# A two-network kernel in fp32: kmat's queue, the modulations' places, both convolutions' inverses, and a guard at the layer fronts

## The chip, the cores and the metric

The kernel runs as one launch on one core of a Trainium2 chip. The metric is the device time of that core in microseconds. The kernel before has a median of 1523.81 us over three runs (1521.16 to 1525.88).

## The reference

Two networks of two layers each follow one another on a sequence of 256 tokens of width 1024, all in fp32. Every layer has a mixer and a feed-forward part, each behind an RMS norm that is modulated by vectors (`sh`, `sc`, `g`) computed from a conditioning vector `c`.

```python
sh1, sc1, g1, sh2, sc2, g2 = split(silu(c) @ mod_w[i] + mod_b[i], 6)
h = modulate(rms_norm(x, norm_g), sh1, sc1)
x = x + g1 * mixer(h)
h = modulate(rms_norm(x, norm_g'), sh2, sc2)
x = x + g2 * ffn(h)

# network 1, layer 0: s5_mixer (state space) beside moba_attention, then @ ab_w_out
# network 1, layer 1: conformer_conv
def conformer_conv(h, w_in, b_in, dw_w, dw_b, ln_g, ln_b, w_out, b_out):
    a = h @ w_in + b_in
    a = a[..., :D_CONV] * jax.nn.sigmoid(a[..., D_CONV:])
    a = causal_dwconv(a, dw_w, dw_b)          # 31 taps
    a = jax.nn.silu(layer_norm(a, ln_g, ln_b))
    return a @ w_out + b_out
# network 2, layer 0: latent attention over the tokens and a context of 256 more
# network 2, layer 1: hyena_mixer
    y = (two_sided_fftconv(v, h_fwd, h_bwd) + v * d_bias) * x1
    return y @ w_out + b_out
```

## The kernel before, in words

Activations are kept transposed, as eight chunks of 128 channels by 256 tokens. Each weight arrives in tiles of 128x1024 fp32 (512 KB) and is split: ACT writes a rounded high part `hi` (L412), DVE the rest `lo` (L413). A product is then three matmuls, hi by hi, hi by lo and lo by hi (`mm3`, L434 to L436). A block of 128 output channels is 8 chunks by 3, so 24 matmuls of 256 columns. TensorE therefore works through blocks, each of which waits for its weight's two parts.

SP's queue loads the weights in a fixed order into pools of buffers (`raw` with five, and `raw2` where `more` opens a second pool). A load waits in that order until the tile that used its buffer has been split, and all loads behind it wait too. POOL's queue loads rows of a second form of the modulation weights (`modt`) into `mraw`, three buffers, for DVE, which forms products of a row by `c` (`also`, L506). The rest of the modulation is done by TensorE: `modulation` loads a tile of two 128-row slices and issues four matmuls on it into one bank `mo` (L532). The planner has lists of such pending steps (`later`), each with a cost, and the code around a block counts `done` upward (`behind`, `fill`, `need`); `pace` sets how often DVE's row products come.

Which instruction stands where on an engine is decided when the program is built: the tile framework orders them by a simulated schedule, and `tc.issue_after` forbids it to take an instruction before another one. On the chip each engine runs its order as written.

The stages, in the order of time, are: conditioning and input of the first network, with the state space `ssm` and its block matrix `kmat` (made in `ktab`, sent to DRAM as `kd`, read back as `kmat`), the attention heads and `ssm_out`, `ab_out`; `ffn1` (gate0, up0, down0); the convolution layer `layer_cm` (cm_in, a 256-point transform by matmuls, its inverse, cm_out); `ffn1` again; the context's operand and latent; `layer_mla`; `ffn2`; `layer_hy`; `ffn2`. A `Front` stands at the start of each layer: the first block is multiplied before the norm's scale is known, and `stats` supplies the scale through `rsqrt` (L633 to L638), a chain of eleven tiny DVE steps.

## Time and profile before

| what | value |
|---|---|
| median of 3 runs | 1523.81 us |
| profiled execution | 1522.47 us, its span 1520.7 us |
| granted TensorE clock over the span | 0.959 of full speed |
| PE busy | 1379.3 us (91%) |
| DVE busy | 1195.9 us (79%) |
| ACT busy | 839.3 us (55%) |
| POOL busy | 125.1 us (8%) |
| moved by DMA | 311.9 MB, 205 GB/s on the mean |

The profiled execution is 1.8 us longer than its span, and 1.3 us shorter than the median. Busy times of the engines overlap. The clock is the share of full speed (2.4 GHz) that was granted to TensorE: a stretch with 0.50 ran at 1.2 GHz.

### The profile page before, as it was taken

The numbers are of one execution on the slowest core, as the hardware profiler recorded it, in microseconds if no ns is written. First come the engines' busy times: TensorE is split into PE (matmuls) and PEld (weight loads), VectorE is DVE, ScalarE is ACT, GpSimd is POOL, SyncE is SP. The second block draws the span as 40 slices with busy tenths as digits, with TensorE's granted clock in tenths as the row PEclk, the third lists the DMA queues.
The fourth block names the chain that finished last, engine by engine and source line by source line (L and its number), as shares of the span: only waits on it lengthen the run. The fifth ranks groups of instructions, "written<-read, shape, count | busy, mean of one in ns | idle before, by whom it ended". The sixth has DMA issues, their size and how long they took to land.

```text
span 1520.7 us, 28172 instructions
## 1 busy us (share of the span) xinstructions
PE 1379.3 (91%) x10686; PEld 1249.7 (82%) x10686; DVE 1195.9 (79%) x2428; ACT 839.3 (55%) x1562; POOL 125.1 (8%) x166
## 2 busy tenths in 40 slices
PE   6969879999988689989987998989999999889997
PEld 3638779999973689989986877989998678889997
DVE  7958869978674678787968876899886979799954
ACT  5416466554452467554545765766545654676642
POOL 1000100101000000000100651000010000000000
PEclk9969989999999799998988999999999999999998
DMA  9476766878669246775835243467695664556651
GB/s 363 167 160 211 240 233 212 286 250 303 237 231 364 76 156 187 237 240 187 321 90 186 84 140 124 143 200 249 213 353 181 247 237 138 164 167 211 205 171 39
DMA packets 96214, 311.89 MB, mean 205 GB/s; under 512 B 14533, under 2 KB 18222, under 8 KB 95950
## 3 DMA queue, kind: packets, MB, share of 16 engines
q1 hardware_dynamic: 77054, 244.01, 48.7%
q0 software_dynamic: 17856, 65.02, 13.1%
q8 instruction: 84, 1.38, 0.4%
q10 hardware_dynamic: 1168, 1.06, 0.3%
q14 instruction: 52, 0.43, 0.1%
HBM read 308.73 MB, written 1.32 MB: 204 GB/s over the span
## 4 chain that ended last, share of the span: by engine, by line
PE 59%; issue 27%; DVE 6%; DMA 4%; ACT 2%; POOL 1%; SPq 0%; DVEq 0%; POOLq 0%; ACTq 0%
PE mm L434 16%; PE mm L436 16%; PE mm L435 16%; DVE lo L413 2%; PE o L1512 1%; POOL mraw L504 1%; DMA raw<-gate 1%; PE mo L532 1%; ACT hi L412 1%; PE ax L1612 1%; DMA kmat<-kd 1%; DVE mraw L506 1%; PE sx L1496 0%; PE s L434 0%; PE ax L1496 0%
## 5 line engine op out<-in xcount | busy, mean ns | idle before, releaser
L412 ACT ACTIVATE hi<-raw 128x1024 fp32r<-128x1024 f32 (+3 forms) x402 | 403.7, 1008 | 406.0 <-PE mm L435 285.3
L413 DVE TENSOR_TENSOR lo<-raw,hi 128x1024 fp32r<-128x1024 f32 (+3 forms) x402 | 465.3, 1161 | 167.0 <-ACT hi L412 161.8
L434 PE MATMUL mm<-hh,hi 128*128 128x256 f32 x1472 | 416.9, 287 | 16.4 <-DVE e L758 5.6
L436 PE MATMUL mm<-hh,lo 128*128 128x256 f32 x1472 | 415.5, 283 | 3.0 <-DVE lo L413 3.0
L435 PE MATMUL mm<-hl,hi 128*128 128x256 f32 x1472 | 414.9, 283 | 0.5 <-DVE hl L712 0.5
L434 PEld LDWEIGHTS mm<-hh,hi 128*128 128x128 f32 x1472 | 278.2, 190 | 26.0 <-issue 6.9
L435 PEld LDWEIGHTS mm<-hl,hi 128*128 128x128 f32 x1472 | 280.0, 190 | 5.1 <-DVE hl L712 2.0
L436 PEld LDWEIGHTS mm<-hh,lo 128*128 128x128 f32 x1472 | 279.8, 190 | 4.7 <-DVE lo L413 3.8
L434 PE MATMUL mm<-ah,hi 128*128 128x256 f32 x704 | 200.8, 286 | 1.5 <-ACT hi L412 1.5
L436 PE MATMUL mm<-ah,lo 128*128 128x256 f32 x704 | 198.6, 284 | 3.8 <-DVE lo L413 3.8
L435 PE MATMUL mm<-al,hi 128*128 128x256 f32 x704 | 198.3, 282 | 0.0
L434 PE MATMUL mm<-zh,hi 128*128 128x258 f32 x608 | 176.4, 295 | 20.6 <-ACT hi L412 10.9
L436 PE MATMUL mm<-zh,lo 128*128 128x258 f32 x608 | 176.2, 291 | 2.3 <-DVE lo L413 2.3
L435 PE MATMUL mm<-zl,hi 128*128 128x258 f32 x608 | 176.2, 291 | 0.0
L504 POOL DMA_DIRECT2D mraw<-modt x124 | 65.7, 530 | 1230.1 <-DVE mraw L506 1111.1
L506 DVE SCALAR_TENSOR_TENSOR mraw<-mraw,crow 128x1024 f32<-128x1024 f32 x124 | 149.9, 1219 | 6.3 <-DMA mraw<-modt 6.2
L434 PEld LDWEIGHTS mm<-zh,hi 128*128 128x128 f32 x608 | 118.9, 197 | 23.2 <-ACT hi L412 11.7
L436 PEld LDWEIGHTS mm<-ah,lo 128*128 128x128 f32 x704 | 132.6, 189 | 4.8 <-DVE lo L413 4.4
L434 PEld LDWEIGHTS mm<-ah,hi 128*128 128x128 f32 x704 | 133.3, 189 | 3.1 <-ACT hi L412 1.9
L435 PEld LDWEIGHTS mm<-al,hi 128*128 128x128 f32 x704 | 133.4, 190 | 1.0 <-issue 1.0
L436 PEld LDWEIGHTS mm<-zh,lo 128*128 128x128 f32 x608 | 119.7, 197 | 2.9 <-DVE lo L413 2.9
L435 PEld LDWEIGHTS mm<-zl,hi 128*128 128x128 f32 x608 | 120.6, 199 | 0.0
(416 smaller groups left out, 2076.4 us busy)
## 6 DMA issues: line engine op xcount, KB each, us to landing
raw<-up SPq DMA_DIRECT2D x132, 512.0 KB, 4.0
mraw<-modt POOLq DMA_DIRECT2D x124, 512.0 KB, 5.2
raw<-down SPq DMA_DIRECT2D x64, 512.0 KB, 4.6
raw<-mod SPq DMA_DIRECT2D x60, 512.0 KB, 6.2
raw<-gate SPq DMA_DIRECT2D x44, 512.0 KB, 4.7
raw<-down SPq DMA_DIRECT2D x32, 384.0 KB, 3.5
raw<-hy_in SPq DMA_DIRECT2D x24, 512.0 KB, 6.8
raw<-cm_in SPq DMA_DIRECT2D x16, 512.0 KB, 5.5
```

The lines of the kernel that those rows point to most:

```text
L412: nc.scalar.activation(hi, src, AF.Copy)
L413: return nc.vector.tensor_tensor(lo, src, hi.bitcast(F32), op=ALU.subtract)
L434: nc.tensor.matmul(out, wh, xh, start=start, stop=False)
L435: nc.tensor.matmul(out, wh, xl, start=False, stop=False)
L436: self.last = nc.tensor.matmul(out, wl, xh, start=False, stop=stop)
L504: nc.gpsimd.dma_start(w, self.d[f"modt{layer}"][u])
L506: nc.vector.scalar_tensor_tensor(w, w, 1.0, row, op0=ALU.mult, op1=ALU.mult, accum_out=out[:, u : u + 1]))
L532: nc.tensor.matmul(acc[g * 32 : g * 32 + 32, :], wt, src, start=(g not in begun), stop=last)
L1512: nc.tensor.matmul(o[i * 64 : i * 64 + 64], vals[:, k, c : c + 64], pt[i][:, k, :], start=(k == 0), stop=(k == 3))
L1612: nc.tensor.matmul(ps, m[:, k, m0 : m0 + P], src[:, k, s], start=(k == 0), stop=(k == 1))
```

## The change

- `kd` and `kmat` are sent through POOL's queue, and `ssm_out` is issued after the second pair of heads (`c == 1`) instead of the first, behind the last matmul.
- `more` gives the first five tiles behind it to the first pool, and the filter's loads are issued in the ninth feed-forward pair (`at={8: ...}`).
- The first `later` takes three column blocks instead of two (`range(4, 7)`) and DVE four rows fewer; `pace` and the end of a list reset the counters; the convolution's pairs, a `fill(3)` and the blocks of `down` take the modulations of the later layers.
- In `layer_cm` the transform is cut into `part` generators; parts 0 and 1 are issued behind the input blocks 5 and 7. The mean (`mu`) is not subtracted before the inverse but goes through it: three more matmuls per channel block use it as a broadcast operand. The inverse gives all 256 tokens in one PSUM tile half; z stays in PSUM, four banks.
- In `layer_hy` the inverse gives all 256 tokens from four matmuls of 256 columns instead of two halves of 128 that DVE adds and subtracts.
- `Front.guard` holds the splits of blocks 3 and 4 until the `rsqrt` chain is over.
- `ctx_operand` and `kv_latent` become steps that the feed-forward's pairs 15, 17 and 18 and the blocks of `down` call.
- `stats2` makes both scales in one `rsqrt` of four columns, and the positions' matmul is issued after the last matmul.

TensorE's order around the first matmul on `kmat`, before: `mo` is the modulation's bank and `qr`, `qi`, `X` belong to the state space.

```order
L532 MATMUL mo_1049<-raw_1058,cs_85 32x512 x2
L532 MATMUL mo_1049<-raw_1062,cs_85 32x512 x2
L532 MATMUL mo_1049<-raw_1066,cs_85 32x512 x2
L1089 MATMUL sx_1263<-kmat_867,u2_660 32x128 x4
L1092 MATMUL sx_1263<-qr_288,X_933 32x128 x4
L1092 MATMUL sx_1263<-qi_289,X_933 32x128 x4
```

The same place now; `ssb` is a head's probabilities, `hh` the input operand's high part.

```order
L449 MATMUL mm_1288<-hh_312,lo_1292 128x256
L547 MATMUL mo_1088<-raw_1324,cs_85 32x512 x2
L1216 MATMUL ax_1227<-ident_89,ssb_1214 128x128
L547 MATMUL mo_1088<-raw_1328,cs_85 32x512
L1216 MATMUL ax_1227<-ident_89,ssb_1214 128x128 x2
L547 MATMUL mo_1088<-raw_1328,cs_85 32x512
L1110 MATMUL sx_1396<-kmat_867,u2_660 32x128 x4
L1113 MATMUL sx_1396<-qr_288,X_933 32x128 x4
```

Five input blocks (118 of their matmuls), eight modulation tiles and the first heads' matmuls have moved ahead of it.

SP's order of weight loads between `ab_out` and the first feed-forward, before: `raw` and `raw2` are the two pools, `cmf` and `cmg` the convolution's matrices.

```order
L425 DMA raw_2130<-ab_out 128x1024
L425 DMA raw_2247<-up0 128x1024
L425 DMA raw_2345<-up0 128x1024
L425 DMA raw_2433<-up0 128x1024
L425 DMA raw_2521<-up0 128x1024
L425 DMA raw_2609<-up0 128x1024
L1252 DMA cmf_2185<-k_cm_f 128x384
L1254 DMA cmg_2187<-k_cm_g 128x320
L425 DMA raw2_2196<-gate0 128x1024
```

The same place now.

```order
L438 DMA raw_2134<-ab_out 128x1024
L438 DMA raw_2190<-gate0 128x1024
L438 DMA raw_2241<-up0 128x1024
L438 DMA raw_2273<-gate0 128x1024
L438 DMA raw_2339<-up0 128x1024
L438 DMA raw_2383<-gate0 128x1024
L438 DMA raw_2471<-gate0 128x1024
L438 DMA raw_2559<-gate0 128x1024
L438 DMA raw2_2427<-up0 128x1024
```

The first gate weight now follows `ab_out`'s last one at once, and the filter's loads stand a dozen loads later.

TensorE's order between the convolution's input and its inverse now: `cmat` and `cmau` are the transform's operands, `cmY` its result, `cmmu` the mean.

```order
L1334 MATMUL mm_5483<-cmat_4715,cmf_2877 128x128
L1343 MATMUL mm_5494<-cmau_4716,cmf_2877 128x128
L547 MATMUL mo_5413<-mraw_5497,cs_85 32x512 x2
L547 MATMUL mo_5413<-raw_5501,cs_85 32x512 x2
L547 MATMUL mo_5413<-raw2_5505,cs_85 32x512 x2
L547 MATMUL mo_5413<-mraw_5509,cs_85 32x512 x2
L547 MATMUL mo_5413<-raw_5513,cs_85 32x512 x2
L547 MATMUL mo_5413<-raw2_5517,cs_85 32x512 x2
L1363 MATMUL mm_5524<-cmg_2879,cmY_4718 128x256 x2
L1363 MATMUL mm_5524<-cmg_2879,cmY_4718 128x32
```

Before, 28 modulation tiles stood in one run ahead of the last input blocks of the convolution; six of them are here now, two before, the rest behind.

The diff, cut to its core:

```diff
--- before.py
+++ after.py
+    def guard(self):
+        return self.net.tc.issue_after(self.chain.ins) if self.n in (3, 4) else nullcontext()
     def block(self, ps, wh, wl, evac):
...
     def room(self):
+        if self.hold:
+            self.hold -= 1
+            return self.raw.tile([P, 1024], F32, name="raw")
         self.turn = (self.turn + 1) % len(self.raws)
...
             self.step()
+        if not self.pending:
+            self.done = 0.0
...
         self.sums(st, 2, sq2)
-        v1 = self.t([P, 2], "nv")
-        v.tensor_scalar(v1, st[:, 0:2], 1.0 / D, EPS, op0=ALU.mult, op1=ALU.add)
-        y1 = self.rsqrt(v1)
-        v2 = self.t([P, 2], "nv")
-        v.tensor_tensor(v2, y1, y1, op=ALU.mult)
...
-        y2 = self.rsqrt(v2)
-        v.tensor_tensor(y2, y2, y1, op=ALU.mult)
+        a = self.t([P, 4], "nv4")
+        v.tensor_scalar(a[:, :2], st[:, 0:2], 1.0 / D, EPS, op0=ALU.mult, op1=ALU.add)
+        v.tensor_scalar(a[:, 2:], st[:, 2:4], 1.0 / D, None, op0=ALU.mult)
+        v.scalar_tensor_tensor(a[:, 2:], a[:, :2], EPS, a[:, 2:], op0=ALU.mult, op1=ALU.add)
+        y = self.rsqrt(a, 4)
+        y1, y2 = y[:, :2], y[:, 2:]
         yield None
...
             self.raws.append((p, "raw2"))
+            self.hold = 5
             yield
...
-    def down(self, w, hi, lo, evac, every=1.0):
+    def down(self, w, hi, lo, evac, every=1.0, then=None):
         self.pace(every)
-        self.linear(w, range(Front.late), hi, lo, evac)
+        for m in range(Front.late):
+            self.linear(w, [m], hi, lo, evac)
+            if then:
+                self.behind(then)
         self.pace(1000.0)
...
         for q in range(4):
-            nc.sync.dma_start(kd[:, q, :, :].rearrange("s h m -> h s m"), kt[q * 32 : q * 32 + 16, :, :])
+            nc.gpsimd.dma_start(kd[:, q, :, :].rearrange("s h m -> h s m"), kt[q * 32 : q * 32 + 16, :, :])
         kmat = sp.tile([P, 32, P], F32, name="kmat")
...
         for j in range(8):
-            nc.sync.dma_start(kmat[j * 16 : j * 16 + 16, :, j * 16 :],
+            nc.gpsimd.dma_start(kmat[j * 16 : j * 16 + 16, :, j * 16 :],
                               kd.rearrange("s q h m -> h (s q) m")[:, :, : (8 - j) * 16])
...
                 cur = nxt
-                if c == 0:
-                    yc, yh, yl = self.ssm_out(sp, ap, u2)
+                if c == 1:
+                    with self.tc.issue_after(self.last.ins):
+                        yc, yh, yl = self.ssm_out(sp, ap, u2)
...
                 self.linear(d["cm_in"], [8 + j], hi, lo, gate)
+                if j in (5, 7):
+                    self.behind(parts[j == 7])
                 self.linear(d["cm_in"], [j], hi, lo, val)
-            for j in range(8):
-                pair(j)
+                if j in (5, 7):
+                    self.behind(parts[j == 7])
             Y = cp.tile([P, 3, D], F32, name="cmY")
-            parts = ((0, 512), (512, 896), (896, 1024))
...
+            def part(n, a, b):
                 s = slice(a, b)
-                vr, vi, vs = (self.mm()[:, : b - a] for _ in range(3))
-                for i, (q, x_) in enumerate(((vr, at[:, 1, s]), (vi, at[:, 0, s]), (vs, au[:, s]))):
-                    last = nc.tensor.matmul(q, cf[:, i, :], x_, start=True, stop=True)
+                vr, vi = (self.mm()[:, : b - a] for _ in range(2))
+                for i, (q, x_) in enumerate(((vr, at[:, 1, s]), (vi, at[:, 0, s]))):
+                    nc.tensor.matmul(q, cf[:, i, :], x_, start=True, stop=True)
...
                                            accum_out=su[:, i, n : n + 1])
+                yield
+                vs = self.mm()[:, : b - a]
+                self.last = nc.tensor.matmul(vs, cf[:, 2, :], au[:, s], start=True, stop=True)
                 v.scalar_tensor_tensor(Y[:, 2, s], vs, 1.0, H[:, 2, s], op0=ALU.mult, op1=ALU.mult,
                                        accum_out=su[:, 2, n : n + 1])
-            self.fill(2, last)
+                yield
+            parts = [part(n, a, b) for n, (a, b) in enumerate(((0, 512), (512, 896), (896, 1024)))]
+            for j in range(8):
+                pair(j)
+            for _ in parts[2]:
+                pass
+            self.fill(3, self.last)
...
             v.tensor_scalar(mu, mu, -1.0 / D, None, op0=ALU.mult)
-            for n in range(2):
-                s = slice(n * 512, n * 512 + 512)
-                for i in range(3):
-                    if (n + i) % 2:
-                        v.tensor_scalar(Y[:, i, s], Y[:, i, s], mu[:, i : i + 1], None, op0=ALU.add)
-                    else:
-                        nc.scalar.activation(Y[:, i, s], Y[:, i, s], AF.Identity, bias=mu[:, i : i + 1])
-            z = cp.tile([P, 8, T], F32, name="cmz")
+            zs = [z[:, i * T : i * T + T] for z in [self.mm() for _ in range(4)] for i in range(2)]
+            ins = ((0, slice(0, T), slice(0, T)), (1, slice(0, T), slice(T, 2 * T)), (2, slice(0, 32), slice(2 * T, 2 * T + 32)))
             q = []
             for j in range(8):
...
-                od = self.t([P, T], "eo", 2, pool=cp)[:, :P]
-                nc.scalar.activation(od, ps[:, :P], AF.Identity, bias=db[:, j : j + 1])
-                v.tensor_tensor(z[:, j, :P], ps[:, P:T], od, op=ALU.add)
-                v.scalar_tensor_tensor(z[:, j, : P - 1 : -1], ps[:, P:T], db2[:, j : j + 1], od, op0=ALU.add, op1=ALU.subtract)
-                self.sumsq(q, z[:, j, :], j, DC)
-            r = self.rstd(q, D, 1, 0)
+                for i, o, c in ins:
+                    nc.tensor.matmul(zs[j][:, o], Y[:, i, j * P : (j + 1) * P], cg[:, c], start=(i == 0), stop=False)
+                for i, o, c in ins:
+                    nc.tensor.matmul(zs[j][:, o], mu[:, i : i + 1].to_broadcast([P, P]), cg[:, c], start=False, stop=(i == 2))
+                self.sumsq(q, zs[j], j, DC, bias=db[:, j : j + 1])
+            r_ = self.rstd(q, D, 0, 2)
...
             zh, zl = self.operand()
...
             self.sumsq(cq, cx[k], k, DC, pool=cxp)
-        r = self.rstd(cq, D)
+        stats = self.stats(cq, D)
+        self.behind(stats)
+        yield
+        with self.tc.issue_after(self.last.ins):
+            r = next(stats)
         for k in range(DC):
             t = self.t([P, T], "n2", pool=cxp)
-            nc.vector.scalar_tensor_tensor(t, cx[k], gc[:, k : k + 1], r, op0=ALU.mult, op1=ALU.mult)
+            nc.vector.scalar_tensor_tensor(t, cx[k], g[:, k : k + 1], r, op0=ALU.mult, op1=ALU.mult)
             nc.scalar.activation(ch[:, k, :], t, AF.Identity, bias=sh[:, k : k + 1])
...
                 kp = self.ring("o")[:, s]
-                nc.tensor.matmul(kp, self.rsum[:64, :], pe[:64, s], start=True, stop=True)
+                with self.tc.issue_after(self.last.ins):
+                    nc.tensor.matmul(kp, self.rsum[:64, :], pe[:64, s], start=True, stop=True)
                 for i in range(4):
...
             for j in range(8):
-                ps = self.mm()
...
+                ps = self.mm()[:, :T]
+                for k in range(4):
+                    nc.tensor.matmul(ps, Y[:, k, j * P : (j + 1) * P], gg[:, k, :], start=(k == 0), stop=(k == 3))
                 y = self.t([P, T], "e")
-                od = self.t([P, P], "eo", 2, pool=hp)
-                nc.scalar.activation(od, pb, AF.Copy)
-                v.tensor_tensor(y[:, :P], pa, od, op=ALU.add)
-                v.tensor_tensor(y[:, : P - 1 : -1], pa, od, op=ALU.subtract)
-                v.tensor_tensor(y, y, x1[:, j, :], op=ALU.mult)
+                v.tensor_tensor(y, ps, x1[:, j, :], op=ALU.mult)
                 self.split(yh[:, j, :], yl[:, j, :], y)
...
                         pass
-            self.later(0, self.modulation(0, range(4, 6), cs, mods[:1]), 1.5)
+            self.later(0, self.modulation(0, range(4, 7), cs, mods[:1]), 1.5)
             row = self.row(0)
-            self.pace(1.2)
-            self.also(1, 0, 24, 40, row, mods[0])
+            self.pace(1.0)
+            self.also(1, 0, 28, 40, row, mods[0])
             self.p1 = per.tile([P, d["par1"].shape[1]], F32, name="p1")
...
-        self.ffn1(0, x, f, None, six(0, 5), sq, mid=mid, front=f2)
+        self.ffn1(0, x, f, None, six(0, 5), sq, mid=mid, front=f2, at={8: lambda: next(cm)})
         self.dump("x1", x)
...
         self.later(4, self.modulation(1, range(6, 9), cs, mods[1:2]), 2.5)
-        self.later(5, self.modulation(2, range(4), ("c_2", "c_ctx_2"), (mods[2], modc)), 5.0)
+        self.later(5, self.modulation(2, range(4), ("c_2", "c_ctx_2"), (mods[2], modc)), 2.0)
         self.pace(2.0)
...
                     self.also(7, 2, 24, 40, row2[0], mods[2])
-                    gc = self.gain("a2c", modc[:, 8:16], self.par("norm_mix_g_2", 0, 8))
-                    self.ctx_operand(cxp, ch, cl, gc, modc[:, 0:8])
-                    for _ in self.kv_latent(ch, cl, ckh, ckl, pe, 0, kv0, cxp, self.ax):
-                        pass
+                    next(latent)
+                    self.behind(latent)
...
                 with self.more(4):
-                    self.ffn1(1, x, f, None, six(1, 5), sq, sq2, lat, context, f2)
+                    self.ffn1(1, x, f, None, six(1, 5), sq, sq2, lat, context, f2, {j: lambda: next(ctx) for j in (15, 17, 18)}, latent)
```

## Rows read from the trace of the kernel before

**Rows 1.** busy us of each engine by stretch (us), then granted clock, DMA share, GB/s

```profile
0.00:1520.70 1520.70, 1379.29 (x10686) 1249.69 (x10686) 1195.94 (x2428) 839.30 (x1562) 125.12 (x166) 0.96 0.62 205
76.00:209.00 133.00, 103.37 (x930) 84.02 (x924) 93.67 (x226) 56.90 (x119) 9.76 (x18) 0.87 0.72 213
85.00:101.00 16.00, 1.01 (x12) 0.23 (x8) 9.40 (x35) 0.00 (x0) 0.00 (x0) 0.59 1.11 141
101.00:112.00 11.00, 11.00 (x114) 6.37 (x107) 3.23 (x3) 3.66 (x4) 0.00 (x0) 0.51 0.82 289
186.00:200.00 14.00, 4.06 (x19) 3.56 (x19) 9.27 (x19) 5.92 (x12) 2.66 (x5) 0.65 0.99 355
440.00:476.00 36.00, 27.89 (x147) 7.50 (x145) 7.99 (x28) 5.48 (x15) 1.58 (x3) 1.00 0.98 378
489.00:518.00 29.00, 15.03 (x75) 12.23 (x73) 20.77 (x78) 8.96 (x24) 0.00 (x0) 0.76 0.26 87
545.00:570.00 25.00, 20.86 (x149) 20.20 (x148) 17.24 (x43) 14.24 (x31) 0.00 (x0) 0.86 0.35 119
673.00:697.00 24.00, 15.96 (x106) 15.28 (x105) 15.82 (x43) 11.08 (x20) 0.53 (x1) 0.79 0.45 156
770.00:815.00 45.00, 32.37 (x197) 28.82 (x197) 34.51 (x102) 22.51 (x51) 3.69 (x7) 0.81 0.43 148
1268.00:1281.00 13.00, 9.52 (x61) 8.54 (x60) 13.00 (x31) 4.75 (x13) 1.20 (x3) 0.80 0.61 177
600.00:630.00 30.00, 30.00 (x255) 30.00 (x254) 23.23 (x39) 17.34 (x27) 1.58 (x3) 1.00 0.74 240
499.70:503.50 3.80, 3.77 (x18) 3.77 (x18) 0.54 (x2) 1.21 (x2) 0.00 (x0) 0.50 0.00 0
```

**Rows 2.** waits of the span: waiter <- releaser: us in total, times, longest us

```profile
PE sx L1089 <- DMA kmat<-kd: 15.0, 1, 15.0
PE sx L644 <- DVE ny L638: 18.6, 6, 6.2
```

**Rows 3.** timeline of SP's DMA issues, 62 to 100 us: start us, us, engine line op

```profile
82.59 1.77 SPq L992 DMA_DIRECT2D kd<-ktab  x4
87.15 8.25 SPq L996 DMA_DIRECT2D kmat<-kd  x8
```

**Rows 4.** tile kmat: its DMAs

```profile
DMA to landing us min/median/max: 5.9/7.2/8.4
```

**Rows 5.** the page: modulation rows, then a queue's packets, MB, share of engines

```profile
L504 POOL DMA_DIRECT2D mraw<-modt x124 | 65.7, 530 | 1230.1 <-DVE mraw L506 1111.1
L506 DVE SCALAR_TENSOR_TENSOR mraw<-mraw,crow 128x1024 f32<-128x1024 f32 x124 | 149.9, 1219 | 6.3 <-DMA mraw<-modt 6.2
q0 software_dynamic: 17856, 65.02, 13.1%
```

**Rows 6.** waits of PE, 60 to 215 us

```profile
PE mm L434 <- ACT hi L412: 10.9, 2, 9.8
```

**Rows 7.** DMA issues, 160 to 210 us: KB each, median us to landing

```profile
raw<-gate SPq DMA_DIRECT2D x7, 512.0 KB, 16.6
```

**Rows 8.** timeline of PE, 442.5 to 478 us

```profile
442.57 4.50 PE L532 MATMUL mo<-raw,cs 128*32 128x512 f32 x40
461.85 1.05 PE L532 MATMUL mo<-raw,cs 128*32 128x512 f32 x4 [0.22 <-DMA raw<-mod]
```

**Rows 9.** timeline of PE, 494 to 506 us

```profile
499.73 3.78 PE L1338 MATMUL mm<-cmg,cmY 128*128 128x128 f32 x16 [3.51 <-ACT cmY L1331]
```

**Rows 10.** timeline of DVE, 550 to 560 us

```profile
551.61 0.16 DVE L653 TENSOR_SCALAR nv<-sx 128x2 f32<-128x2 f32 x1 [2.44 <-PE sx L624]
551.88 1.23 DVE L413 TENSOR_TENSOR lo<-raw,hi 128x1024 fp32r<-128x1024 f32 x1
558.21 0.15 DVE L638 SCALAR_TENSOR_TENSOR ny<-nu,ny 128x2 f32<-128x2 f32 x1
```

More of the change, by code (lines that the diff above doesn't have):

```diff
@@ L327, in block @@
                 r = next(self.stats)
+                if self.n == 0:
+                    self.chain = net.chain
             if self.n:
@@ L355, in __init__ @@
         self.dbg = dbg or {}
-        self.turn = 0
+        self.turn = self.hold = 0
         self.ahead = False
@@ L445, in linear @@
                 if front.first():
-                    front.block(ps, *self.wsplit(w[mb]), partial(evac, mb))
+                    with front.guard():
+                        wh, wl = self.wsplit(w[mb])
+                    front.block(ps, wh, wl, partial(evac, mb))
                     continue
@@ L571, in pace @@
     def pace(self, every):
-        self.every = every
+        self.every, self.dotted = every, 0.0
     def dot(self):
@@ L626, in sums, with rsqrt @@
         return last
-    def rsqrt(self, v):
+    def rsqrt(self, v, n=2):
         nc = self.nc
-        y = self.t([P, 2], "ny")
-        u = self.t([P, 2], "nu")
+        y, u = (self.t([P, n], nm + (str(n) if n > 2 else "")) for nm in ("ny", "nu"))
         nc.vector.tensor_scalar(u.bitcast(I32), v.bitcast(I32), 1, None, op0=ALU.logical_shift_right)
@@ L687, in stats2, with sumsq @@
         yield r[:, :T]
-    def sumsq(self, sq, src, k, n, scale=1.0, pool=None):
+    def sumsq(self, sq, src, k, n, scale=1.0, pool=None, **bias):
         nc = self.nc
@@ L801, in ffn1 @@
                 mid()
-            self.down(d[f"down{l}"], ah, al, self.residual(x, g2, sq, None, sq2, pool, front))
+            self.down(d[f"down{l}"], ah, al, self.residual(x, g2, sq, None, sq2, pool, front), then=then)
     def ffn2(self, l, x, hi, lo, g2, sq, mid, front=None):
@@ L1269, in layer_cm @@
             cf, cg, H = cmf
-            db, db2, bm = (cp.tile([P, n], F32, name=nm) for nm, n in (("cmdb", 8), ("cmdb2", 8), ("cmbm", 1)))
+            db, bm = (cp.tile([P, n], F32, name=nm) for nm, n in (("cmdb", 8), ("cmbm", 1)))
             ps = self.ax()
@@ L1378, in kv_latent, with ctx_operand @@
         yield
-    def ctx_operand(self, cxp, ch, cl, gc, sh):
+    def ctx_operand(self, cxp, ch, cl, modc):
         nc, d = self.nc, self.d
+        self.need(5)
+        g = self.gain("a2c", modc[:, 8:16], self.par("norm_mix_g_2", 0, 8))
+        sh = modc[:, 0:8]
         cx = []
@@ L1656, in layer_hy @@
             x1 = hx.tile([P, 8, T], F32, name="x1")
+            gg = hx.tile([P, 4, T], F32, name="gg")
+            nc.sync.dma_start(gg, d["k_hy_g"])
             Y = hyp.tile([P, 4, D], F32, name="Y", tag="hsd")
@@ L1823, in run @@
             with self.tc.tile_pool(name="cx", bufs=1, reuse_waits="tile") as cxp:
+                ch, cl = (self.zp.tile([P, DC, T], F32R, name=n, tag=t) for n, t in (("ch", "zh"), ("cl", "zl")))
+                ctx = self.ctx_operand(cxp, ch, cl, modc)
+                latent = self.kv_latent(ch, cl, ckh, ckl, pe, 0, kv0, cxp, self.ax)
                 def context():
-                    ch = self.zp.tile([P, DC, T], F32R, name="ch", tag="zh")
-                    cl = self.zp.tile([P, DC, T], F32R, name="cl", tag="zl")
                     self.need(6)
```

44 lines of the change are left out of this document (18 added, 26 removed).

## The prediction

> **What bounds the kernel now.** I read the busy times of the windows first, the whole span at their head: PE is busy for 1379.3 of 1520.7 us (91%) and DVE for 1195.9 (79%) [rows 1]. PE sets the pace, and a share of DVE work that high means that a PE wait which goes can leave a DVE wait in its place. PE is idle for 141 us, and the granted clock is 0.96 on the mean. In the stretches with 0.50 it is at 1.2 instead of 2.4 GHz; (1 − 0.96) × 1520.7 = 61 us is what full clock throughout would return. So about 200 us can be had without removing work. A steady stretch of PE shows none of that: 30.00 us busy in 30 us at clock 1.00 with 255 matmul records [rows 1], or 0.118 us for a 256-column matmul. Everything then depends on the few windows in which PE stands still; the waits and the timelines of these say who holds it.
>
> **The change part by part.** All sums go against the profiled execution, 1522.5 us, which is 1.3 us under the median of the runs.
>
> *A, kmat.* From 85 to 101 us PE is busy 1.0 of 16 us, and from 101 to 112 us it runs at clock 0.51 [rows 1], so that 11.0 busy us hold 5.6 us of full-speed work. The wait is 15.0 us for the DMA of kmat [rows 2]; SP issued kd at 82.6 and kmat from 87.15 on, for 8.25 us [rows 3], each landing 7.2 us after its issue [rows 4], and the input weights behind them in SP's order came late too. At most 15 + 5.4 = 20 us are to be had. The change puts the twelve DMAs into POOL's order, behind three modulation rows, and the matmuls on kmat behind five more input blocks, two attention chunks' first heads and eight modulation tiles: some 118 matmuls of 0.118 us (14 us) and 8 tiles of 0.45 us (3.6, see C), with small ones about 20 us. PE gets there at 85 + 20 = 105 us or later. POOL's launch of a row costs 0.53 us [rows 5]; at that price kd and kmat take 12 × 0.53 = 6.4 us, and with two landings kmat is there near 82.6 + 6.4 + 2 × 7.2 = 103 us: just hidden. Upper bound of the cost: software DMA packets took 13.1% of 16 × 1520.7 us for 17856 packets [rows 5], 0.18 us each; kmat has 8 × 16 × 32 = 4096 rows, and at that price they take 4096 × 0.18 / 16 = 46 us, landing near 135. Launch and descriptors of so fine a pattern on POOL are not in the trace, so both ends stay. I take the launch price, since these rows are short. POOL's later modulation rows come after kmat, and DVE's fourth row product waits for them in DVE's order; but four products of 1.22 us [rows 5] become eight tiles on PE.
>
> *B, the first gate weights.* From 186 to 200 us PE is busy 4.1 of 14 us at clock 0.65 [rows 1], its longest wait 9.8 us for the hi part of a weight [rows 6], while gate weights take 16.6 us to land against 512 KB each [rows 7]. They sat in the second weight pool, whose memory comes free only with ab_out's last matmul, and behind two filter loads in SP's order. After, the first five come into the first pool right behind ab_out's. Gain 8 to 12.
>
> A and B together: 133 us from 76 to 209. PE's busy time of 103.4 us falls by 5.4 + 1.4 of half clock and rises by 3.6 for the tiles, to 101; DVE has 93.7 − 4 × 1.2 = 89. With 7 us for waits on a DVE that is then 82% full that is 108: 25 us gained, 14 from A and 11 from B. Range −5 to +31.
>
> *C, modulations at one place.* From 440 to 476 us PE works off 28 tiles, DMA share 0.98 at 378 GB/s [rows 1]. Resident tiles go at 4.50 us for 40 records, 10 tiles, 0.45 each; the ones waited for take 1.05 + 0.22 = 1.28 us [rows 8], which is the DMA's time. Ten at 0.45 and eighteen at 1.28 with the closing steps make the 33 us beside 3 us of projection. The new order has two tiles at a time in the convolution's pairs, six in a fill, four behind the statistics, and sixteen in cm_out and gate1: 28 × 0.45 = 12.6, for broken groups 14. One new wait: the fill's fourth tile is loaded behind a cm_out weight, whose slot its own second tile frees; it costs 3 us (0 if the slot is free early, 6.2 if the DMA queue is busy as in the windows above). 33 − 14 − 3 = 16, range 8 to 19.
>
> *D, convolution.* From 489 to 518 us: 29 us, PE busy 15.0 at clock 0.76 [rows 1]; the mean's subtraction on ACT holds PE 3.5 us [rows 9]. The first two parts go behind input blocks and the mean into the inverse. That adds work: per j four matmuls of 256 fp32 columns and two of 32. A 128-column fp32 matmul is two records; 18 records take 3.77 us at clock 0.50 [rows 1], 0.105 each at full clock, so 0.42 us for 256 columns. Eight j make 8 × (4 × 0.42 + 2 × 0.2) = 16.6 us instead of about 5. I add the statistics and their chain, 9, and the moved parts, 3: 29, no gain. Range −6 to +6. z in PSUM takes all four of the mm banks; cm_out's first block needs the same z anyway.
>
> *E, the fronts.* The rsqrt chain of 11 tiny steps runs from 551.6 to 558.4, 6.8 us, since weight splits of 1.23 us stand between its steps of 0.16 [rows 10]; alone, with the step ahead of them, they are 12 × 0.16 = 1.9, with gaps I take 2.1 (an estimate). PE waits 18.6 us for such chains in six places [rows 2], and the windows show what follows: 545 to 570 idle 4.1 and clock 0.86 [rows 1]. The guard holds two weights of each of six fronts until the chain is done; their splits are then late by at most 2 × 1.2 us, of which three earlier blocks of 24 × 0.118 = 2.8 us hide most. 13 gained of 22 with the clock, range 6 to 20.
>
> *F, the context's operand and latent.* 673 to 697 us: idle 8.0, and clock 0.79 [rows 1] costs 5. Its steps go into three feed-forward pairs and the rest behind down's blocks; DVE's share there is 66%. Gain 9 (6 to 12).
>
> *G, one rsqrt of four columns for two.* 770 to 815 us: idle 12.6, clock 0.81 [rows 1]. One chain of 2.1 us goes, the positions' matmul comes later. 6 (3 to 10).
>
> *H, hyena's inverse.* 64 records of 128 columns become 64 of 256: 6.7 us more on PE; the 13 − 9.5 = 3.5 us of idle PE and the clock loss of 0.20 × 13 us [rows 1] mostly go, and the 16 tiles behind it are spread. −1 (−6 to +4).
>
> Sum: 25 + 16 + 0 + 13 + 9 + 6 − 1 = 68. PE has then some 20 us more to do and 88 us less to wait, of 200. Each new gap of a DVE at 79% takes some back; I book an eighth, 8 us. 1522.5 − 60 = 1462.5, or 1463 with the median's offset.
>
> **A rule against part A.** Before, kmat's eight DMAs left SP in 8.25 us and landed in 7.2 [rows 3, 4]. The Trainium skill ("SBUF — State Buffer", "SBUF: two separate sides") says that a DMA issued from GpSimd has its descriptors written by that engine, which is locked out of a port shared with VectorE while VectorE runs a two-port operation, and advises SP or ACT as issuers. No run here shows it for such a fine pattern; the modulation rows launched in 0.53 us beside a busy DVE [rows 5] speak against it for coarse ones. By the rule kmat would land late, which is the first rival.
>
> **The rivals.**
> 1. kmat late: POOL's twelve DMAs take the 46 us worked out above or more. PE stands from 107 to 135 us, 28 us with half clock behind it, A turns from +14 to −13: 1463 + 27 = 1490. For it: 4096 short rows, a path that no row of before shows. Against: DMA share 0.82 and 1.11 near there did not keep SP's from landing in 7.2 us.
> 2. DVE takes over: it is at 89 of 108 us in A and B, 72% in D, 69% in E; with every chain and split in one order, half of the gain comes back. 1522.5 − 34 = 1490. For it: the windows' DVE columns. Against: DVE loses about 16 us of work (products, z copies, one chain).
> 3. Slower: POOL's descriptors cost so much that kmat holds PE for longer than everything else gains. The place is the same matmul, the other parts give 46 us, so it decides from a landing at 107 + 46 + 20 = 173 us, that is 20 ns for each of 4096 rows behind kd. At 30 ns: 123 us, landing near 213, PE idle 106 instead of 20: 1522.5 − 46 + 86 = 1563. Against: a coarse launch of 128 rows costs 4 ns a row [rows 5].
> 4. The edits change the order but the waits move along: SP stays in order, and every tile that waits for a slot holds a weight behind it. As 1.28 against 0.45 us for all 28 tiles that takes 23 us, with E and F halved another 11 and G gone 6: 20 us left, 1502.
>
> **How the numbers follow.** Forecast 0.62, at 1463 with its own range 1440 to 1484; rival 1 0.12; rival 2 0.12; rival 3 0.04; rival 4 0.10. The range 1432 to 1501 takes in the first two rivals, at the low end the forecast without the 8 us of discount and with two thirds of the 34 us by which the parts' upper ends stand above what I took (1463 − 8 − 23), and the near half of rival 4. About 0.3% (4.6 us) is what a measurement can tell from no change. Slower: rival 3 and a tail of 4, 0.05; same: the same tail, 0.04; faster 0.91.
>
> **What would show it.** After: no PE wait for kmat above 2 us, and clock 1.00 from 85 to 112; PE waits under 3 us at the first gate block; no run of modulation tiles with a DMA share of 0.98; one wait of about 3 us in the fill; the inverse at 16 to 18 us of PE without a hole; 11 chain steps in 2.1 us with no split between, and under 8 us in all of PE's waits for them. The prediction is wrong if PE waits for kmat at all for over 10 us, if the span's PE idle plus clock loss falls by less than 60 us, or if DVE's busy share goes over 85%.

## The result, and the profile after

The changed kernel has a median of 1466.2 us over four runs (1461.7 to 1474.5), the kernel before 1524.2 us. The ratio is 0.963, with a 95% interval of 0.958 to 0.967. Measured again beside the first experiments, it was 1468.7 us and 0.964 (0.961 to 0.967). The forecast was 1463, with a range of 1432 to 1501.

The profiled execution took 1474.5 us (the slowest of its four), its span 1472.7 us. Its windows, with the columns of [rows 1]:

```profile
0.00:1472.70 1472.70, 1379.92 (x10750) 1253.52 (x10750) 1178.49 (x2371) 834.02 (x1544) 131.99 (x174) 0.97 0.65 212
85.00:101.00 16.00, 10.82 (x77) 8.69 (x77) 14.13 (x45) 1.39 (x3) 7.90 (x14) 0.89 0.75 130
140.00:165.00 25.00, 18.30 (x116) 12.92 (x110) 14.80 (x35) 15.72 (x34) 0.53 (x1) 0.80 0.44 146
186.00:200.00 14.00, 14.00 (x120) 14.00 (x119) 10.36 (x27) 7.65 (x13) 1.31 (x2) 1.00 0.82 268
```

PE's busy time is what it was, 1380 us, in a span 48 us shorter, with the clock at 0.97 instead of 0.96. Where PE stood from 85 to 101 us [rows 1] it is busy for 10.8 of 16 us, with DVE at 14.1. The first gate block runs without a gap (186 to 200 us). But from 140 to 165 us PE idles for 6.7 us at clock 0.80. Four of PE's waits after, in the form of [rows 2]:

```profile
PE mm L447 <- DVE qk L423: 5.2, 1, 5.2
PE sx L660 <- DVE ny L654: 4.2, 2, 2.5
PE o L1225 <- ACT pt L1218: 3.5, 2, 3.2
PE ax L1216 <- DVE ssb L1213: 3.4, 1, 3.4
```

The wait for kmat is gone and the waits for the rsqrt chains fell from 18.6 to 4.2 us [rows 2]. The other three stand where PE used to wait for kmat (94 us) and behind it (147 and 151 us): for a split of `qk`, for the heads' softmax (`pt`, `ssb`).

The marks at which stages begin, as the start of each one's first matmul in the timelines (us), show which parts paid:

| stage | before | after | after, repeated | stretch up to it changed by (repeated) |
|---|---|---|---|---|
| first matmul on kmat | 100.7 | 120.4 | 122.0 | |
| ab_out | 163.4 | 170.8 | 170.5 | |
| front 1 (gate0) | 196.4 | 191.7 | 190.4 | −6.0 |
| front 2 (convolution) | 398.9 | 388.6 | 388.6 | −4.3 |
| convolution's inverse | 499.7 | 459.3 | 457.7 | −31.7 |
| front 3 | 542.5 | 518.7 | 517.0 | +16.5 |
| latent attention | 764.6 | 734.8 | 728.4 | −10.7 |
| front 5 | 948.3 | 912.9 | 907.4 | −4.7 |
| front 6 (hyena) | 1151.4 | 1108.4 | 1102.1 | −8.4 |
| front 7 | 1305.4 | 1266.4 | 1259.0 | +2.9 |
| last matmul | 1513.4 | 1466.5 | 1459.2 | −7.8 |

Up to `ab_out` the changed kernel is 7 us later than before, although a wait of 15 us is gone; it is ahead at front 1 mostly by part B (with B undone front 1 comes at 195.0 us). The stretch up to the convolution's inverse gains 32 us, and the one behind it gives 16 back.

From 76 us to `ab_out`'s first matmul PE idles about as long as before, 17.8 against 16.8 us (the kernel before, then the changed one):

```profile
76.00:163.40 87.40, 70.65 (x687) 53.33 (x681) 63.89 (x172) 39.29 (x89) 3.70 (x7) 0.86 0.72 188
76.00:170.80 94.80, 77.00 (x730) 58.18 (x731) 66.88 (x178) 39.10 (x88) 11.94 (x21) 0.90 0.63 193
```

The answers to the other rows of before follow. kmat on POOL's queue [rows 3, 4]:

```profile
84.65 2.15 POOL L1013 DMA_DIRECT2D kd<-ktab  x4 [44.60 <-DVE tx L1080]
90.36 4.97 POOL L1017 DMA_DIRECT2D kmat<-kd  x8 [3.56 <-DMA kd<-ktab]
```

```profile
DMA to landing us min/median/max: 4.5/7.9/10.6
```

The eight launches take 0.62 us each, and a median of 7.9 us to land, against 7.2 from SP.

A front's chain on DVE, as in [rows 10], now runs from 526.9 to 529.2 us, 2.3 us, with the splits behind it:

```profile
526.89 0.16 DVE L669 TENSOR_SCALAR nv<-sx 128x2 f32<-128x2 f32 x1 [4.91 <-PE sx L641]
529.05 0.16 DVE L654 SCALAR_TENSOR_TENSOR ny<-nu,ny 128x2 f32<-128x2 f32 x1
529.13 2.36 DVE L423 TENSOR_TENSOR lo<-raw,hi 128x1024 fp32r<-128x1024 f32 x2
```

The end of the fill and the convolution's inverse on PE (start us, us, engine line op, names, shapes, count; in brackets the idle time ahead):

```profile
454.31 1.07 PE L547 MATMUL mo<-mraw,cs 128*32 128x512 f32 x2
457.72 1.68 PE L547 MATMUL mo<-raw,cs 128*32 128x512 f32 x8
459.33 2.22 PE L1363 MATMUL mm<-cmg,cmY 128*128 128x256 f32 x10
476.78 1.27 PE L1363 MATMUL mm<-cmg,cmY 128*128 128x256 f32 x6 [0.93 <-ACT n L708]
477.88 1.25 PE L1365 MATMUL mm<-cmg,cmmu 128*128 128x256 f32 x6
```

The six tiles of the fill run without a wait from 454.3 to 459.3 us, 0.83 us each where I had 0.45, and the inverse runs from 459.3 to 479.1 us, 19.8 us with two waits of 0.93 us in it. The windows of the fill and of the inverse:

```profile
454.30:459.30 5.00, 5.00 (x25) 0.99 (x24) 1.59 (x12) 0.00 (x0) 0.53 (x1) 0.53 0.62 189
459.30:479.10 19.80, 17.94 (x102) 16.04 (x98) 2.55 (x6) 2.99 (x7) 0.00 (x0) 1.00 0.39 140
```

The fill ran at a granted clock of 0.53, so near the lower level of 1.2 GHz, where the ten tiles of before had 1.00 [rows 1, 8]: that is why a tile took nearly twice as long. PE had stood for 2.55 us ahead of the last transposition just before.

### The profile page after: what moved, and what is told of

Its sections match the earlier page's. It is cut to its first block, busy times and chain, and to the rows that moved or that the text cites. A ratio compares the mean times of both kernels' runs of the same rounds, so it can differ in the third digit from the quotient of the medians.

```text
span 1472.7 us, 28204 instructions
## 1 busy us (share of the span) xinstructions
PE 1379.9 (94%) x10750; PEld 1253.5 (85%) x10750; DVE 1178.5 (80%) x2371; ACT 834.0 (57%) x1544; POOL 132.0 (9%) x174
## 4 chain that ended last, share of the span: by engine, by line
PE 29%; issue 13%; DVE 4%; ACT 2%; DMA 1%; POOL 1%; DVEq 0%; POOLq 0%; ACTq 0%
PE mm L447 7%; PE mm L449 7%; PE mm L448 7%; DVE lo L423 1%; PE o L1545 1%; PE ax L1645 1%; PE mm L1714 1%; ACT hi L422 1%; PE s L447 1%; PE s L448 1%; PE s L449 0%; PE mo L547 0%; PE ax L1529 0%; DMA mraw<-modt 0%; POOL mraw L519 0%
## 5 line engine op out<-in xcount | busy, mean ns | idle before, releaser
L447 PE MATMUL mm<-hh,hi 128*128 128x256 f32 x1472 | 420.2, 289 | 23.2 <-DVE qk L423 5.2
L521 DVE SCALAR_TENSOR_TENSOR mraw<-mraw,crow 128x1024 f32<-128x1024 f32 x120 | 144.8, 1217 | 3.8 <-DMA mraw<-modt 3.8
L448 PEld LDWEIGHTS mm<-zl,hi 128*128 128x128 f32 x608 | 117.6, 194 | 0.4 <-issue 0.4
```

What stands on the lines that cost most here:

```text
L447: nc.tensor.matmul(out, wh, xh, start=start, stop=False)
L448: nc.tensor.matmul(out, wh, xl, start=False, stop=False)
L521: nc.vector.scalar_tensor_tensor(w, w, 1.0, row, op0=ALU.mult, op1=ALU.mult, accum_out=out[:, u : u + 1]))
```

## The experiments

Each was timed in five rounds, unless said, against the kernel before on the same chip. Differences to the changed kernel are differences of these ratios times 1524 us; their uncertainty is about 6 us. The same difference taken between two medians, which can come from different chips, is up to 4 us off from this; where a span is given, it is from both.

**The changed kernel again.**

> The changed kernel itself once more, on the chip of the three runs beside it, as their base: both theories expect a ratio to the kernel before of 0.960 to 0.966. It also shows how far the marks of its profile (first gate block at 191.7 us, inverse of the convolution at 459.3, end at 1466.5) repeat: both theories expect them within 3 us at the gate block.

1468.7 us, ratio 0.964 (0.961 to 0.967); the gate block at 190.4 us.

**Part A undone.** In the changed kernel:

```diff
-            nc.gpsimd.dma_start(kd[:, q, ...
+            nc.sync.dma_start(kd[:, q, ...
...
-                if c == 1:
-                    with self.tc.issue_after(self.last.ins):
-                        yc, yh, yl = self.ssm_out(sp, ap, u2)
+                if c == 0:
+                    yc, yh, yl = self.ssm_out(sp, ap, u2)
...
-            self.later(0, self.modulation(0, range(4, 7), cs, mods[:1]), 1.5)
+            self.later(0, self.modulation(0, range(4, 6), cs, mods[:1]), 1.5)
...
-            self.pace(1.0)
-            self.also(1, 0, 28, 40, row, mods[0])
+            self.pace(1.2)
+            self.also(1, 0, 24, 40, row, mods[0])
```

The eight DMAs of kmat move to `nc.sync` in the same way.

> The changed kernel with part A undone: kd and kmat on SP, ssm_out after the first heads, two column blocks of modulations and sixteen row products there. Theory 1 (from the profile after): part A gives nothing, since what PE waited for at kmat it now waits for at DVE's state-space steps and at the heads' chain; the first gate block comes at 188 to 193 us as in the changed kernel (191.7) and the time is within 4 us of it, ratio 0.959 to 0.966. Rival (the prediction's term): A gives 14 us, so the gate block comes near 206 and the ratio is about 0.972.

1463.9 us, ratio 0.962 (0.959 to 0.964), 4 us less than with part A, so no difference that the runs can tell; the gate block at 191.6 us. Its windows:

```profile
85.00:101.00 16.00, 12.14 (x88) 9.94 (x89) 13.58 (x45) 1.26 (x2) 0.53 (x1) 0.89 1.02 120
76.00:192.00 116.00, 97.74 (x886) 78.48 (x884) 87.71 (x217) 50.64 (x108) 9.70 (x18) 0.90 0.69 203
```

PE is busy for 12.1 us from 85 to 101 us without part A, and begins on kmat from SP at 103.1 us after 1.4 us of idle time: from 42 us on SP's order now has four input weights and four modulation tiles ahead of kd, where the kernel before had one and five. So the other edits, by SP's order the planner's, remove the wait alone, and the stage is still no shorter. Theory 1's times hold and the rival falls, but theory 1's reason is only half of it. What held the end of the stage here is the modulation (`mod`) for the front's operand `zh`, which DVE completes after the last of its row products. The rows are that step in the kernel before, without part A and with it, then PE's wait without part A:

```profile
190.02 0.18 DVE L508 TENSOR_TENSOR mod<-mod,p 128x16 f32<-128x16 f32 x1
190.60 0.17 DVE L523 TENSOR_TENSOR mod<-mod,p 128x16 f32<-128x16 f32 x1
180.33 0.16 DVE L523 TENSOR_TENSOR mod<-mod,p 128x12 f32<-128x12 f32 x1
```

```profile
PE mm L447 <- ACT zh L307: 6.3, 1, 6.3
```

Without part A PE begins `ab_out` at 163.8 us, 6.6 earlier than with it (170.5), and then waits 6.3 us for `zh`. With part A there are four row products fewer and the modulation is ready 10 us earlier, but PE comes later. The two nearly cancel.

**Part A alone, in the kernel before.** The reverse of the diff above, in the kernel before.

> The kernel before with part A alone: kd and kmat through POOL's queue, ssm_out after the second heads, a third column block of modulations on TensorE and four row products fewer. Theory 1: PE's wait of 15 us for kmat was not on the path that set the end of the stage (DVE's in-order state-space steps, weight splits and the heads' chain set it), so the wait goes and the first gate block comes within 4 us of the 196.4 us of before; ratio 0.997 to 1.003. Rival (the prediction's term): 14 us earlier, ratio 0.991.

1531.6 us, ratio 1.004 (1.002 to 1.007): slower, and the gate block comes at 207.0 us in the profiled execution (span 1540.3 us, above the median), 10.6 later. Both expectations are missed, theory 1's by 7 us. POOL's rows, the landing there, and PE's costliest wait from 60 to 200 us:

```profile
85.70 2.15 POOL L992 DMA_DIRECT2D kd<-ktab  x4 [45.88 <-DVE tx L1059]
94.84 5.00 POOL L996 DMA_DIRECT2D kmat<-kd  x8 [6.99 <-DMA kd<-ktab]
```

```profile
DMA to landing us min/median/max: 9.6/11.0/12.5
```

```profile
PE mo L532 <- DMA raw<-mod: 5.4, 3, 3.3
```

kd lands later and kmat takes a median of 11.0 us, while DMA's share in that stretch is 0.85; PE no longer waits for kmat, as its matmuls stand later in its order. It waits for modulation tiles instead. Which of these makes the 10.6 us is not shown.

**Twelve row products left out** (three rounds). The modulation columns 28 to 40 of the first layer are zero, so what follows is not the reference's result.

```diff
-            self.also(1, 0, 28, 40, row, mods[0])
+            v.memset(mods[0][:, 28:40], 0.0)
```

> The changed kernel without the twelve row products on DVE that stand between the state space and ab_out (the modulation columns 28 to 40 of the first layer are set to zero instead). Theory 1a: DVE's work in its order is what bounds the stretch from 85 to 190 us; without 12 x 1.22 = 14.6 us of it the first gate block comes 8 us or more earlier than in the changed kernel (190.4), near 180. Theory 1b: the heads' back and forth between engines bounds it, and the gate block moves by less than 4 us. The time follows: ratio 0.957 to 0.959 by 1a, 0.962 to 0.965 by 1b.

1454.6 us, ratio 0.954 (0.950 to 0.957); the gate block at 180.6 us, 9.8 earlier. The stage up to it, with the products (first row) and without:

```profile
76.00:190.40 114.40, 96.40 (x936) 77.06 (x927) 86.13 (x214) 52.48 (x111) 13.50 (x24) 0.91 0.66 206
```

```profile
76.00:180.60 104.60, 93.22 (x877) 74.72 (x870) 69.81 (x184) 51.24 (x110) 7.12 (x12) 0.92 0.57 166
```

DVE's 86 us go to 70, and the stage shrinks by 9.8: DVE's work in its order limits it, as theory 1a has it. The edit also takes twelve loads of 512 KB out of the stretch (DMA share 0.66 to 0.57). None of PE's longer waits there was for a DMA, in the changed kernel or in this one, which speaks for DVE, but no run parts the two. The kernel as a whole gained 14 to 16 us, somewhat more than the stage, which is within the uncertainty.

**Part B undone.**

```diff
-            self.hold = 5
...
+        next(cm)
...
-        self.ffn1(0, x, f, None, six(0, 5), sq, mid=mid, front=f2, at={8: lambda: next(cm)})
+        self.ffn1(0, x, f, None, six(0, 5), sq, mid=mid, front=f2)
```

> The changed kernel with part B undone: the first tiles behind the second weight pool go to either pool in turn, and the filter's loads are issued ahead of the feed-forward. Both theories expect PE to wait 8 to 11 us at the first gate block again, and 8 to 11 us more in all (ratio 0.969). Rival: the moved order of part A has already taken the wait away, and less than 3 us come.

1477.0 us, ratio 0.969 (0.967 to 0.971), 7 us more than the changed kernel, just under the expected 8 to 11. PE waits again:

```profile
PE mm L444 <- ACT hi L422: 8.0, 2, 7.0
```

**Part C's planner edits undone.**

```diff
-        self.every, self.dotted = every, 0.0
+        self.every = every
...
-        if not self.pending:
-            self.done = 0.0
...
-        self.later(5, self.modulation(2, range(4), ("c_2", "c_ctx_2"), (mods[2], modc)), 2.0)
+        self.later(5, self.modulation(2, range(4), ("c_2", "c_ctx_2"), (mods[2], modc)), 5.0)
```

> The changed kernel with part C's planner edits undone (the counters aren't reset at the end of a list or by pace, the context's modulation is due at 5.0 a step instead of 2.0); the fill of three and the calls behind the blocks stay. The prediction's term: 16 us slower (8 to 19), ratio about 0.975, with a run of modulation tiles at a DMA share near 1 ahead of the convolution's end. Rival: a fill and the calls alone spread them, so under 6 us come (ratio under 0.968).

1497.0 us, ratio 0.983 (0.980 to 0.985), 28 us more: above the range that I gave for it. The tiles are drained in one run again, at DMA's pace:

```profile
443.00:473.00 30.00, 25.01 (x122) 4.88 (x120) 1.47 (x6) 2.21 (x7) 0.00 (x0) 1.00 0.92 360
```

```profile
PE mo L547 <- DMA raw<-mod: 3.6, 13, 0.9
```

The convolution's inverse begins 99.5 us after front 2, against 69.1 in the changed kernel: 30 us. Another 7 us are lost by front 1 (197.4 us), where the planner's reset also orders SP's loads: from 47 us on it has six modulation tiles in a row ahead of the next input weight, where the changed kernel has two.

**Part D undone.** Transform, mean and inverse of the convolution as in the kernel before (with its `fill(2)`; the trace has six tiles there all the same).

> The changed kernel with part D undone: the convolution's transform, mean and inverse as in the kernel before (128 tokens of each half, mean subtracted by ACT and DVE, z in SBUF), all else as changed. The prediction's term for D: 0 (from 6 us worse to 6 us better), ratio 0.960 to 0.968. Rival 1: the parts behind input blocks hide the transform and D is worth over 6 us, ratio over 0.968. Rival 2: twelve more us of matmuls in the inverse outweigh it, ratio under 0.960.

1455.9 us, ratio 0.953 (0.950 to 0.956), 17 us less than the changed kernel: rival 2. From front 2 to the inverse and from there to front 3, with part D (two rows) and without it (two rows), then the old inverse's first and last matmuls:

```profile
388.60:457.70 69.10, 63.43 (x464) 53.83 (x462) 53.83 (x131) 36.39 (x76) 1.48 (x2) 0.95 0.55 175
457.70:517.00 59.30, 49.86 (x349) 43.00 (x345) 32.58 (x74) 25.91 (x55) 3.69 (x7) 0.96 0.66 225
```

```profile
389.50:454.00 64.50, 59.56 (x463) 52.90 (x462) 54.20 (x134) 37.15 (x78) 2.54 (x4) 1.00 0.57 183
454.00:503.00 49.00, 39.76 (x289) 35.20 (x289) 36.21 (x91) 27.75 (x64) 2.64 (x5) 0.86 0.69 239
```

```profile
454.07 3.44 PE L1359 MATMUL mm<-cmg,cmY 128*128 128x128 f32 x16 [1.95 <-ACT cmY L1352]
461.56 0.33 PE L1361 MATMUL mm<-cmg,cmY 128*128 128x64 f32 x2
```

The old inverse takes 7.8 us, the new one 19.8. And the stretch ahead of it, where two parts of the transform were to hide behind input blocks, is 64.5 us without hiding and 69.1 with it. PE idles there for 5.7 us with part D and 4.9 without: its waits moved and did not go. With part D it stands for 2.55 us at the last transposition, for DVE, which has the parts' products and a weight split ahead in its order (first row). The clock of the stretch is 0.95 against 1.00. The six tiles of the fill behind that stop take 5.0 us, as shown above; without part D they take 2.8 us at clock 1.00 (second row).

```profile
450.23 0.54 PE L1259 MATMUL ax<-ident,eo 128*128 128x128 f32 x2 [2.55 <-DVE eo L1255]
449.30:452.20 2.90, 2.83 (x26) 0.68 (x24) 2.90 (x13) 0.00 (x0) 1.58 (x3) 1.00 0.19 38
```

**The mean's matmuls taken once.** In the changed kernel, a row of the mean is made first and added by one matmul per channel block:

```diff
-                for i, o, c in ins:
-                    nc.tensor.matmul(zs[j][:, o], mu[:, i : i + 1].to_broadcast([P, P]), cg[:, c], start=False, stop=(i == 2))
+                if j == 0:
+                    mb, mr = self.ax(), cp.tile([P, T], F32, name="cmmr")
+                    for i, o, c in ins:
+                        nc.tensor.matmul(mb[:, o], mu[:, i : i + 1].to_broadcast([P, P]), cg[:, c], start=(i == 0), stop=(i == 2))
+                    nc.scalar.activation(mr[:1], mb[:1, :T], AF.Copy)
+                nc.tensor.matmul(zs[j], self.ones[:1, :].to_broadcast([1, P]), mr[:1], start=False, stop=True)
```

> The changed kernel with the mean's way through the inverse taken once: the three matmuls on the mean give one row of 256 tokens, ACT copies it, and each of the eight channel blocks adds it by one matmul over one partition. Theory: the inverse is bound by PE at 0.42 us for 256 fp32 columns; 8 x (1.04 - 0.42) = 5.0 us of matmuls go and about 1.5 us for the row and its copy come, so the inverse and the time fall by 3 to 4 us. Rival: the squares on ACT and DVE's sums bound the inverse, and nothing changes (within 1 us).

1471.9 us, ratio 0.967 (0.964 to 0.970): no gain. Its window showed why, and the next experiment tested it.

**The same over 128 partitions.**

```diff
-                    nc.scalar.activation(mr[:1], mb[:1, :T], AF.Copy)
+                    nc.scalar.activation(mr, mb[:, :T], AF.Copy, scale=D / P)
-                nc.tensor.matmul(zs[j], self.ones[:1, :].to_broadcast([1, P]), mr[:1], start=False, stop=True)
+                nc.tensor.matmul(zs[j], self.onesd, mr, start=False, stop=True)
```

> As x_row, but the row of the mean is kept on 128 partitions and added by a matmul with a full 128 by 128 matrix instead of one over a single partition. x_row's profile had the clock at 0.51 from 463 to 484 us, right after the one-partition matmuls began, where the changed kernel had 0.99. Theory: the clock fell because those matmuls use one row of the array; with full ones it stays at 1.00, the inverse is 3 to 4 us shorter, ratio 0.961 to 0.962. Rival: the wait for the row's copy or the squares stopped PE and brought the clock down; then it is at 0.5 here too and the ratio stays at 0.966.

1460.9 us, ratio 0.957 (0.954 to 0.960), 11 to 15 us less than with the thin matmuls and 8 to 11 less than the changed kernel, more than the 3 to 4 expected. The window of the inverse in the changed kernel, with the row over one partition, and over 128:

```profile
460.00:480.00 20.00, 17.78 (x106) 15.29 (x108) 3.43 (x12) 3.46 (x8) 0.00 (x0) 1.00 0.31 116
```

```profile
460.00:480.00 20.00, 17.17 (x52) 12.26 (x50) 2.55 (x6) 3.46 (x8) 0.00 (x0) 0.59 0.29 103
```

```profile
460.00:480.00 20.00, 15.22 (x89) 11.34 (x87) 5.41 (x22) 5.14 (x14) 1.05 (x2) 1.00 0.54 203
```

The same product over one partition goes with a clock of 0.59, over 128 it stays at 1.00. The three windows do not hold the same work, so the inverse's first and last matmuls, over one partition (two rows) and over 128:

```profile
454.90 2.22 PE L1363 MATMUL mm<-cmg,cmY 128*128 128x256 f32 x10
476.88 1.22 PE L1369 MATMUL mm<-cmmr,ones 1*128 1x256 f32 x2
457.02 2.22 PE L1363 MATMUL mm<-cmg,cmY 128*128 128x256 f32 x10
473.44 0.68 PE L1369 MATMUL mm<-cmmr,onesd 128*128 128x256 f32 x2
```

The inverse takes 23.2 us over one partition, 17.1 over 128, and 19.8 in the changed kernel, so 2.7 us less than there, near the expected. The waits of 0.93 us between its blocks are there in all three, so the rival falls. Where the rest of the 8 to 11 us comes from is not shown.

**The guard undone (part E).**

```diff
-        return self.net.tc.issue_after(self.chain.ins) if self.n in (3, 4) else nullcontext()
+        return nullcontext()
```

> The changed kernel with part E undone: the guard at the fronts holds nothing. The prediction's term: 13 us slower (6 to 20), ratio about 0.973. The stretches between fronts in which nothing else was changed (front 2 from front 1, end from front 7) got 4 and 8 us shorter with the change, which speaks for the upper half, 16 to 20 us and a ratio of 0.975 to 0.977. Rival: the other edits already keep the splits out of the chain, and under 6 us come (ratio under 0.968).

1485.5 us, ratio 0.974 (0.972 to 0.977), 16 us more. The chain of front 3 on DVE, with weight splits between its steps (its first step, the first split, the last step), then PE's waits for what follows a chain, without the guard and with it:

```profile
528.14 0.16 DVE L669 TENSOR_SCALAR nv<-sx 128x2 f32<-128x2 f32 x1 [4.14 <-PE sx L641]
528.41 1.22 DVE L423 TENSOR_TENSOR lo<-raw,hi 128x1024 fp32r<-128x1024 f32 x1
532.75 0.16 DVE L654 SCALAR_TENSOR_TENSOR ny<-nu,ny 128x2 f32<-128x2 f32 x1
```

```profile
PE mm L447 <- DVE n L348: 14.6, 8, 3.3
```

```profile
PE mm L447 <- DVE n L348: 5.4, 4, 3.3
```

The chain takes 4.8 us instead of 2.3, and the waits behind it 14.6 instead of 5.4.

**A, D and H undone together.** The three sets of edits above, and hyena's inverse in two halves of 128 as before.

> The changed kernel with A, D and H undone together (state space's queue and order, the convolution's transform and inverse, hyena's inverse as in the kernel before), keeping B, C, E, F and G. Alone, undoing A gave 0.9615 and undoing D 0.953 against 0.9641. If they add and H is worth -1 to -3: ratio 0.948 to 0.951, about 1447 to 1451 us. Rival: the gains overlap through the order that the planner gives, and it stays at 0.953.

1448.2 us, ratio 0.949 (0.947 to 0.951): the fastest kernel here, 20 to 23 us under the changed one. It lies where the sum puts it; H alone was not run.

**The same with the transform's first parts behind input blocks.**

> As best_a, but the convolution's first two transform parts stay behind the input blocks 5 and 7, with the mean subtracted by ACT and DVE and the old inverse behind them. Theory: in the profile with D undone PE idles 5 us between the transform's parts and their products; hidden, they give 3 to 5 us more than best_a (ratio 0.945 to 0.948). Rival: the parts' products on DVE hold the input blocks back instead, and it is no faster than best_a.

1453.3 us (1443.2 to 1463.0), ratio 0.952 (0.949 to 0.956): no faster than the version without; whether slower stays open. Its inverse begins 70.8 us after front 2 (with eight tiles in the fill), against 64.6 in the version without (with six), so here too nothing was hidden.

## Why the prediction was right, and which of its terms were not

The time came out as forecast, 1466 against 1463, but by terms that missed on both sides. That the sum is so near is luck:

| part | forecast, us | measured by undoing it, us |
|---|---|---|
| A, kmat | +14 | −4, none within the uncertainty (alone in the kernel before: −7) |
| B, gate weights | +11 | +7 |
| C, modulations | +16 | +28 |
| D, convolution | 0 | −17 |
| E, guard | +13 | +16 |
| F, G and H, and C's fill and calls, not undone singly | +14 | about +25, as the rest of 55, if the parts add up |
| discount | −8 | |

Against the forecast A, B and D fell short by 18, 4 and 17 us; C, E, the rest and the discount made up 12, 3, 11 and 8 of these.

- A failed in the step that took PE's idle time at kmat for time on the path. That idle time did not go: up to `ab_out` it is 17.8 us where it was 16.8, now in waits for DVE (13 us) and ACT (5). This is rival 2's mechanism, in the place where I had DVE at 82%. That figure is a mean over the stage; from 85 to 101 us DVE is now busy for 14.1 of 16. A row pointed that way: while PE stood from 85 to 101 us, DVE was busy for 9.4 of the 16 [rows 1], so part of the stall was covered by work that the rest of the stage needs. And with sixteen row products the modulation for the front is ready at 190 us, in the kernel before as with part A undone, so without the stall the gate block could have come at some 191 us instead of 196.4, 5 us earlier and not 14. The price of POOL's launch was right (0.62 against 0.53 us), the landing too, so rivals 1 and 3 fall; but PE came to kmat at 120.4 us, where I had 105 or later.
- B was right in place and nearly in size: the wait came back at 8.0 us, and 7 us of time with it, a little under my 8 to 12.
- C's mechanism was right, its size short by 12. The reset also orders the loads of the first stage (7 us by front 1), which I had not counted with it. The wait at the fill's fourth tile that I charged 3 us for is not in the trace; instead each of the six tiles takes 0.83 us, since the clock was at 0.53, behind a stop of PE that I had not foreseen. With part D undone the same six run at clock 1.00 in 2.8 us.
- D failed in what was to pay for the longer inverse, and in the inverse's size. I had 16.6 us instead of about 5; it took 19.8 (PE busy for 17.9) instead of 7.8. What goes to pay for it (the transform's waits and half of the clock) I took from a 29 us window, and the stretch ahead of the inverse, in which the parts were to hide, is 4.6 us longer with them than without: nothing was hidden.
- E held: the chain takes 2.3 us.
- PE's idle time with the clock's loss fell from 141 + 61 to 93 + 43 us, 66 less, where the prediction wanted 60 at least. Of its other signs the clock from 85 to 101 us (1.00 wanted) is 0.89, and 0.79 in the repeat.
- Two sums of the prediction are slightly off: 103.4 − 6.8 + 3.6 is 100, not 101 us, and rival 2's 1522.5 − 34 is 1488.5, not 1490. Neither moves the forecast by more than 1 us.

## What to carry to other kernels

A stall of the busiest engine is worth its length only if the end of the stage waits for that engine: before pricing it, find what the next stage's first instruction needs and when the other engines deliver it. Here that was a modulation behind sixteen row products on DVE, ready at 190 us with the stall and without it. Work that is added to the bound engine to free another is paid in full, and what it frees pays only where it was waited for. Several edits that come as one are best undone one by one: here one of the eight made the kernel slower, one gained nothing that the runs can tell, and without these two and a third it runs at 0.949 instead of 0.964.

## What the runs showed of the hardware

Eight matmuls over a single partition among full ones went with a granted clock of 0.59 from 460 to 480 us, where the same product over 128 partitions had 1.00. The inverse took 23.2 against 17.1 us, and a pair of records of that product 1.22 against 0.68 us: the thin form lost the time that it was to save. The span's clock says the same in all six runs of each, 0.964 to 0.972 against 0.973 to 0.978.

The transfers of kmat from POOL landed in a median of 7.9 us beside a DVE that was busy for 14.1 of 16 us, against 7.2 from SP in the kernel before and 7.0 from SP with part A undone; in the kernel before with part A alone it was 11.0. The Trainium skill ("SBUF — State Buffer", "SBUF: two separate sides") has descriptors written by GpSimd wait while VectorE holds the shared port. By these medians that rule could have cost 1 to 4 us here (an estimate), which decides nothing; whether the port or the other transfers made these microseconds no run tells apart.
